# Reciprocal roots by GpSimd's power and one Newton step, squares summed into fewer tiles, last sample columns added on VectorE

## The chip, the cores and the metric

The kernel runs on one core of a Trainium2 chip. The metric is the device time of one execution in microseconds (us), lower being better. The engines in what follows are TensorE (PE; its weight loads are listed apart as PEld), VectorE (DVE), ScalarE (ACT), GpSimd (POOL) and SyncE (SP), which issues most DMAs.

## The reference

One step of a decoder with two layers of width 1024, over 512 prompt columns and 32 sample columns (8 sequences of 4 tokens). Layer 0 mixes with a gated linear attention (GLA), layer 1 with a forgetting attention (FoX) over keys and values that are projected once, between the layers.

```python
def rmsnorm(x, g):
    y = x * lax.rsqrt(jnp.mean(x * x, axis=-1, keepdims=True) + NORM_EPS)
    return y * g
def modulate(x, g, shift, scale):
    return rmsnorm(x, g) * (1 + scale[:, None, :]) + shift[:, None, :]
...
for layer in range(2):
    u = modulate(h, g_norm[layer, 0], ...); h = h + 0.5 * gate0 * swiglu(u, w_up0, w_down0)
    u = modulate(h, g_norm[layer, 1], ...); h = h + gate1 * mixer(u)
    u = modulate(h, g_norm[layer, 2], ...); h = h + 0.5 * gate2 * swiglu(u, w_up1, w_down1)
    if layer == 0:
        kvf = modulate(h, g_kv, ...) @ w_kvf      # then k = rmsnorm(k per head), v, logf
```

Reciprocal roots are needed for the adaptive norms (one set from the inputs and five from `h` after each block that follows; the norm of the shared keys and values and the one that opens layer 1 read the same `h` and share a set), and per head for the GLA output, the keys and the queries.

## The kernel before

The residual stream `h` lies in SBUF as 128 partitions x 8 blocks x 544 columns: the features are on partitions, the 512 prompt and 32 sample tokens are columns. The columns are worked in two halves of 272; the second ends with the 32 sample columns. Weights come from HBM in fp32 and are split into a high part (a cast on ScalarE) and a low part (a subtraction on VectorE, L158); every product is three matmuls (L176, L177, L178).

A feed-forward part ends with its last down projection, whose blocks run over `m` = 0 to 7 for the first half and then for the second. `residual` adds each block to `h` (VectorE, L393); in the second half the sample columns have gates of their own: `gs` on VectorE (L396), then the sum on GpSimd (L398). After the last contribution to a block, `square` squares its half on ScalarE (L346). The squares of blocks 1 to 5 are added on GpSimd (L350) to the tile of block 0; those of blocks 6 and 7 stay as tiles of their own. An output projection (`gwo` after GLA, `fwo` after FoX) ends in the same way.

When the eighth block of a half is there, `after` calls `stats`: matmuls with the tiles of squares as weights and a column of ones (L359) give the sums over the features, one token per partition, in three pieces (128, 128, 16 columns that count). `mean_eps` scales (L328, the tile `nx`), `rsqrt` takes the reciprocal root on VectorE (`nry`, `nrw`): an integer guess from the bits and three Newton steps, twelve instructions. `spread` puts each root on a diagonal (L336, `diag`, VectorE), and matmuls with ones (L337, `rb`) spread it over the partitions. From `rb` (copied to SBUF on ScalarE), `make_u` makes the next operand in two parts, `uh` (ScalarE) and `ul` (VectorE), block by block.

`norm_heads` normalises keys and queries per head: squares on ScalarE, a reduction and scaling on VectorE (`hss`, L1022 to L1024), `rsqrt` for 8 heads of a token block (`h8y`, `h8w`) or 2 of the samples (`h2y`), a product on VectorE (L1026) and one with the gain on GpSimd (L1027, `hxk`). It is called ten times for the keys and ten for the queries. The projection of keys and values (`kv`, L566 to L568) has the sample columns apart: `kv_s` (L554) with `us`, which GpSimd makes (L378).

Each engine runs its own queue in order; the order is fixed when the program is built, by a scheduler that places instructions by its own estimates of durations. SyncE's queue issues the loads of the weights, many blocks ahead.

Of the kernel before, what the change touches and what calls it, by code (L numbers as in the profile page):

```python
# [9 lines left out]
F32 = mybir.dt.float32  # L10
F32R = mybir.dt.float32r
BF16 = mybir.dt.bfloat16
I32 = mybir.dt.int32
U8 = mybir.dt.uint8
AF = mybir.ActivationFunctionType
ALU = mybir.AluOpType
AX = mybir.AxisListType

P = 128
D = 1024  # L20
NB = 8
TP = 512
NS = 32
T = TP + NS
# [5 lines left out]
MAGIC = 1597463007.0  # L30
# [69 lines left out]
def trunk_kernel(ctx: ExitStack, tc: tile.TileContext, a, out, dbg=None, stop=None):  # L100
    nc = tc.nc
    V, S, G, PE, SP = nc.vector, nc.scalar, nc.gpsimd, nc.tensor, nc.sync
    dbg = dbg or {}

    keep = ctx.enter_context(tc.tile_pool(name="keep", bufs=1))
# [4 lines left out]
    def mm_bank(name):  # L110
        return pp.tile([P, 512], F32, tag="mm", name=name, bufs=5)

    def aux_bank(name):
        return pp.tile([P, 512], F32, tag="aux", name=name, bufs=2)
# [14 lines left out]
    h = keep.tile([P, NB, T], F32, name="h")  # L129
# [10 lines left out]
    ones = cst[:, C_ONES:C_ONES + 128]  # L140


    def rsqrt(x, n, tag, rows=P):
        y = tmp.tile([P, n], F32, tag=tag + "y", name=tag + "y")
        w = tmp.tile([P, n], F32, tag=tag + "w", name=tag + "w")
        v, w = y[:rows], w[:rows]
        V.tensor_scalar(out=v.bitcast(I32), in0=x.bitcast(I32), scalar1=1, scalar2=None, op0=ALU.logical_shift_right)
        V.tensor_scalar(out=v.bitcast(I32), in0=v.bitcast(I32), scalar1=-1.0, scalar2=MAGIC, op0=ALU.mult, op1=ALU.add)
        V.tensor_scalar(out=x, in0=x, scalar1=-0.5, scalar2=None, op0=ALU.mult)
        for _ in range(3):  # L150
            V.tensor_tensor(out=w, in0=v, in1=v, op=ALU.mult)
            V.tensor_tensor(out=w, in0=w, in1=x, op=ALU.mult)
            V.scalar_tensor_tensor(out=v, in0=w, scalar=1.5, in1=v, op0=ALU.add, op1=ALU.mult)
        return y

    def halves(hi, lo, src):
# [130 lines left out]
    start = ExitStack()  # L287
# [22 lines left out]
    for t in range(5):  # L310
        n = P if t < 4 else NS
        V.tensor_tensor_reduce(out=junk[:n], in0=xt[t][:n], in1=xt[t][:n], scale=1.0, scalar=0.0, op0=ALU.mult, op1=ALU.add, accum_out=ss0[:n, t:t + 1])
    for k in range(NB):
        ps = mm_bank(f"xT{k}")
# [6 lines left out]
    ps = mm_bank("xTs")  # L321
# [4 lines left out]
    def mean_eps(name, src, n):  # L326
        x = tmp.tile([P, n], F32, tag="nx", name=name)
        V.tensor_scalar(out=x[:], in0=src, scalar1=1.0 / D, scalar2=EPS, op0=ALU.mult, op1=ALU.add)  # L328
        return x

    def spread(name, y, pieces):
        diag = tmp.tile([P, 3, P], F32, tag="diag", name=f"diag{name}", bufs=1)
        ps = aux_bank(f"rb{name}")
        b0 = pieces[0][3]
        for i, (col, k, r0, t0, n) in enumerate(pieces):
            V.tensor_scalar(out=diag[:k, i, :n], in0=cst[:k, C_ID + r0:C_ID + r0 + n], scalar1=y[:k, col:col + 1], scalar2=None, op0=ALU.mult)  # L336
            PE.matmul(ps[:, t0 - b0:t0 - b0 + n], lhsT=ones[:k, :], rhs=diag[:k, i, :n], start=True, stop=True)  # L337
        e = pieces[-1][3] + pieces[-1][4]
        S.copy(rb[:, b0:e], ps[:, 0:e - b0])

    accs = {}

    def square(m, half):
        t0, t1 = HALF[half]
        sq = tmp.tile([P, HA], F32, tag="acc" if m == 0 else "sq", name=f"sq{half}_{m}", bufs=2 if m == 0 else 3)
        S.activation(sq[:], h[:, m, t0:t1], AF.Square)  # L346
        if m == 0:
            accs[half] = [sq]
        elif m < NB - 2:
            G.tensor_tensor(out=accs[half][0][:], in0=accs[half][0][:], in1=sq[:], op=ALU.add)  # L350
        else:
            accs[half].append(sq)

    def stats(name, half):
        t0, t1 = HALF[half]
        ps = aux_bank(f"st{name}")
        for i, o in enumerate((0, 128, 144)):
            for j in range(3):
                PE.matmul(ps[:, i:i + 1], lhsT=accs[half][j][:, o:o + 128], rhs=ones[:, 0:1], start=j == 0, stop=j == 2)  # L359
        x = mean_eps(f"nx{name}", ps[:, 0:3], 3)  # L360
        y = rsqrt(x[:], 3, "nr")
        spread(name, y, [(0, P, 0, t0, 128), (1, P, 0, t0 + 128, 128), (2, P, 112, t0 + 256, 16)])

    def scaled(v, half, scale, k):
# [24 lines left out]
    def residual(name, ps, m, half, gate, last):  # L389
        t0, t1 = HALF[half]  # L390
        p1 = min(t1, TP)
        n = p1 - t0
        V.scalar_tensor_tensor(out=h[:, m, t0:p1], in0=ps[:, 0:n], scalar=mods[:, gate + m, 0:1], in1=h[:, m, t0:p1], op0=ALU.mult, op1=ALU.add)  # L393
        if half:
            st = tmp.tile([P, NS], F32, tag="gs", name=f"gs{name}_{m}", bufs=3)
            V.tensor_tensor(out=st[:].rearrange("p (s t) -> p s t", s=8), in0=ps[:, n:n + NS].rearrange("p (s t) -> p s t", s=8),  # L396
                            in1=mods[:, gate + m, 1:9].unsqueeze(2).to_broadcast([P, 8, 4]), op=ALU.mult)
            G.tensor_tensor(out=h[:, m, TP:T], in0=h[:, m, TP:T], in1=st[:], op=ALU.add)  # L398
        if last:
            square(m, half)  # L400

    def after(name, shift, scale):
        def f(half):
            stats(f"{name}{half}", half)
            if half:
                make_u(name, half, shift, scale)
                return []
            return [lambda k=k: make_u(name, half, shift, scale, k, k + 1) for k in range(NB)]
        return f
# [211 lines left out]

    x0 = mean_eps("nx0", ss0[:], 5)
    y0 = rsqrt(x0[:], 5, "n0")
    spread("0a", y0, [(0, P, 0, 0, 128), (1, P, 0, 128, 128)])
    spread("0b", y0, [(2, P, 0, 256, 128), (3, P, 0, 384, 128), (4, 32, 0, 512, 32)])
# [30 lines left out]
    def gla(after_half):  # L656
        W = a["gla_w_in"][0]
        with tc.tile_pool(name="gla", bufs=1) as gp:
# [199 lines left out]
            def normalise(name, po, n):  # L858
                ss = gp.tile([P, 4], F32, tag="oss", name=f"oss{name}", bufs=2)
                for i in range(n):  # L860
                    S.activation(jk, po(i), AF.Square, accum_out=ss[:, i:i + 1])
                V.tensor_scalar(out=ss[:, 0:n], in0=ss[:, 0:n], scalar1=1.0 / 256, scalar2=EPS, op0=ALU.mult, op1=ALU.add)
                y = rsqrt(ss[:, 0:n], n, f"o{n}")
                if len(ons) == 0:
                    on = onb
                else:
                    on = ada_tile(f"on{name}")[:].rearrange("p (h e) -> p h e", h=4)
                ons.append(on)
                for i in range(n):
                    if i % 2:  # L870
                        S.mul(on[:, i], po(i), y[:, i:i + 1])
                    else:
                        V.tensor_scalar(out=on[:, i], in0=po(i), scalar1=y[:, i:i + 1], scalar2=None, op0=ALU.mult)
# [591 lines left out]
```

## Time and profile before

| | us |
|---|---|
| median of three executions | 2459.07 (2456.82 to 2463.04) |
| profiled execution | 2463.23 |
| its span, first to last instruction | 2461.4 |
| TensorE busy / VectorE / ScalarE / GpSimd | 2391.6 / 1235.5 / 783.5 / 289.5 |
| mean granted clock of TensorE | 0.989 of full speed |

The busy times are shares of the span in which an engine executes; instructions of TensorE overlap, so a busy TensorE is not one at its peak. A row of the timeline has start, duration, engine, line, operation, output from inputs, shapes, and in brackets the idle time ahead of it with what ended that. A row of one source line has minimum, median and maximum duration in ns, and the starts of its first and last instruction.

### The profile page before, as it was taken

The numbers are of one execution on the slowest core, as the hardware profiler recorded it, in microseconds if no ns is written. First come the engines' busy times: TensorE is split into PE (matmuls) and PEld (weight loads), VectorE is DVE, ScalarE is ACT, GpSimd is POOL, SyncE is SP. The second block draws the span as 40 slices with busy tenths as digits, with TensorE's granted clock in tenths as the row PEclk, the third lists the DMA queues.
The fourth block names the chain that finished last, engine by engine and source line by source line (L and its number), as shares of the span: only waits on it lengthen the run. The fifth ranks groups of instructions, "written<-read, shape, count | busy, mean of one in ns | idle before, by whom it ended". The sixth has DMA issues, their size and how long they took to land. (4 is left out here: it accounts for less than half of the span.)

```text
span 2461.4 us, 48211 instructions
## 1 busy us (share of the span) xinstructions
PE 2391.6 (97%) x20204; PEld 2244.4 (91%) x20204; DVE 1235.5 (50%) x2823; ACT 783.5 (32%) x1431; POOL 289.5 (12%) x448
## 2 busy tenths in 40 slices
PE   7999999999899999999999999999999799999999
PEld 6999999988879999999979999999896579999999
DVE  6343334557656344344585344434847656444433
ACT  4212222344534213222334322222337444222221
POOL 0000000104302010000220000000325220000000
PEclk9999999999999999999999999999999899999999
DMA  9636454213172646554247323322157742222221
GB/s 308 232 126 231 156 178 133 65 48 96 36 215 60 224 145 230 179 176 154 97 125 233 99 66 109 97 92 69 44 109 196 177 129 74 91 88 93 70 85 54
DMA packets 325519, 319.38 MB, mean 130 GB/s; under 512 B 24607, under 2 KB 276349, under 8 KB 325254
## 3 DMA queue, kind: packets, MB, share of 16 engines
q1 hardware_dynamic: 297958, 293.81, 37.4%
q0 software_dynamic: 13776, 11.87, 2.3%
q10 hardware_dynamic: 13568, 10.62, 1.4%
q8 instruction: 159, 2.61, 0.4%
q14 instruction: 58, 0.48, 0.1%
HBM read 298.17 MB, written 18.38 MB: 129 GB/s over the span
## 5 line engine op out<-in xcount | busy, mean ns | idle before, releaser
L176 PE MATMUL pa<-uh,hua 128*128 128x272 f32 x1408 | 409.5, 291 | 2.0 <-ACT uh L386 2.0
L177 PE MATMUL pa<-ul,hua 128*128 128x272 f32 x1408 | 407.7, 290 | 0.4 <-DVE ul L387 0.2
L178 PE MATMUL pb<-uh,lub 128*128 128x272 f32 x1408 | 407.5, 289 | 0.0
L176 PE MATMUL pd<-gh,hwd 128*128 128x272 f32 x1408 | 407.4, 289 | 0.0
L178 PE MATMUL pa<-uh,lua 128*128 128x272 f32 x1408 | 406.6, 289 | 0.0
L176 PE MATMUL pb<-uh,hub 128*128 128x272 f32 x1408 | 405.5, 288 | 0.0
L177 PE MATMUL pb<-ul,hub 128*128 128x272 f32 x1408 | 405.5, 288 | 0.0
L177 PE MATMUL pd<-gl,hwd 128*128 128x272 f32 x1408 | 405.5, 288 | 0.0
L178 PE MATMUL pd<-gh,lwd 128*128 128x272 f32 x1408 | 405.2, 288 | 0.0
L393 DVE SCALAR_TENSOR_TENSOR h<-pd,mods,h 128x272 f32<-128x272 f32 (+1 forms) x384 | 185.2, 483 | 255.6 <-PE pd L178 254.4
L176 PEld LDWEIGHTS pa<-uh,hua 128*128 128x128 f32 x1408 | 265.3, 188 | 15.1 <-issue 6.0
L176 PEld LDWEIGHTS pd<-gh,hwd 128*128 128x128 f32 x1408 | 265.1, 188 | 2.9 <-issue 2.9
L177 PEld LDWEIGHTS pa<-ul,hua 128*128 128x128 f32 x1408 | 265.7, 189 | 1.4 <-DVE ul L387 1.2
L177 PEld LDWEIGHTS pb<-ul,hub 128*128 128x128 f32 x1408 | 266.1, 189 | 0.0
L178 PEld LDWEIGHTS pb<-uh,lub 128*128 128x128 f32 x1408 | 265.8, 189 | 0.0
L176 PEld LDWEIGHTS pb<-uh,hub 128*128 128x128 f32 x1408 | 265.7, 189 | 0.0
L177 PEld LDWEIGHTS pd<-gl,hwd 128*128 128x128 f32 x1408 | 265.5, 189 | 0.0
L178 PEld LDWEIGHTS pd<-gh,lwd 128*128 128x128 f32 x1408 | 265.4, 188 | 0.0
L178 PEld LDWEIGHTS pa<-uh,lua 128*128 128x128 f32 x1408 | 265.4, 188 | 0.0
L446 DVE TENSOR_TENSOR g<-g,pb 128x272 f32<-128x272 f32 x176 | 77.1, 438 | 346.5 <-PE pb L178 346.3
L157 ACT CAST hua<-rua 128x1024 fp32r<-128x1024 f32 x88 | 92.2, 1048 | 462.9 <-PE pd L177 352.0
L398 POOL TENSOR_TENSOR h<-h,gs 128x32 f32<-128x32 f32 x192 | 69.5, 362 | 1230.7 <-DVE gs L396 1214.6
(497 smaller groups left out, 4173.1 us busy)
## 6 DMA issues: line engine op xcount, KB each, us to landing
adaw<-in_w_ada_dram SPq DMA_DIRECT2D x128, 512.0 KB, 6.2
rua<-in_w_ffn_up_dram SPq DMA_DIRECT2D x88, 512.0 KB, 3.8
rub<-in_w_ffn_up_dram SPq DMA_DIRECT2D x88, 512.0 KB, 3.8
rwd<-in_w_ffn_down_dram SPq DMA_DIRECT2D x88, 512.0 KB, 5.3
adah<-in_w_ada_dram SPq DMA_DIRECT2D x16, 512.0 KB, 7.9
adaw<-in_w_ada_kv_dram SPq DMA_DIRECT2D x16, 512.0 KB, 7.3
s<-in_state_gla_dram SPq DMA_DIRECT2D x16, 512.0 KB, 6.2
kp<-in_cache_k_dram SPq DMA_DIRECT2D x16, 512.0 KB, 5.7
```

The costliest lines, as they stand in the source:

```text
L157: S.copy(hi, src)
L176: PE.matmul(ps, lhsT=wh, rhs=xh, start=first and i == 0, stop=False)
L177: PE.matmul(ps, lhsT=wh, rhs=xl, start=False, stop=False)
L178: PE.matmul(ps, lhsT=wl, rhs=xh, start=False, stop=last and i == n - 1)
L393: V.scalar_tensor_tensor(out=h[:, m, t0:p1], in0=ps[:, 0:n], scalar=mods[:, gate + m, 0:1], in1=h[:, m, t0:p1], op0=ALU.mult, op1=ALU.add)
L398: G.tensor_tensor(out=h[:, m, TP:T], in0=h[:, m, TP:T], in1=st[:], op=ALU.add)
L446: V.tensor_tensor(out=g[:], in0=g[:], in1=pb[:, 0:HA], op=ALU.mult)
```

## The change

The reciprocal root becomes a power of -1/2 on GpSimd, followed by one Newton step of four operations. In the norms (`stats`) that step runs on GpSimd too; elsewhere (start, GLA, keys, queries) on VectorE. In the first half all eight squares end in one tile, in the second seven in one and the eighth apart, and the statistics matmuls are three or six in place of nine. The last sum of the sample columns of a block goes to VectorE.

```diff
+    mhalf = keep.tile([P, 8], F32, name="mhalf")
+    V.memset(mhalf[:], -0.5)
+
-    def rsqrt(x, n, tag, rows=P):
+    def rsqrt(x, n, tag, rows=P, E=None):
+        E = E or V
         y = tmp.tile([P, n], F32, tag=tag + "y", name=tag + "y")
         w = tmp.tile([P, n], F32, tag=tag + "w", name=tag + "w")
         v, w = y[:rows], w[:rows]
-        V.tensor_scalar(out=v.bitcast(I32), in0=x.bitcast(I32), scalar1=1, scalar2=None, op0=ALU.logical_shift_right)
-        V.tensor_scalar(out=v.bitcast(I32), in0=v.bitcast(I32), scalar1=-1.0, scalar2=MAGIC, op0=ALU.mult, op1=ALU.add)
-        V.tensor_scalar(out=x, in0=x, scalar1=-0.5, scalar2=None, op0=ALU.mult)
-        for _ in range(3):
-            V.tensor_tensor(out=w, in0=v, in1=v, op=ALU.mult)
-            V.tensor_tensor(out=w, in0=w, in1=x, op=ALU.mult)
-            V.scalar_tensor_tensor(out=v, in0=w, scalar=1.5, in1=v, op0=ALU.add, op1=ALU.mult)
+        G.tensor_tensor(out=v, in0=x, in1=mhalf[:rows, 0:n], op=ALU.pow)
+        E.tensor_tensor(out=w, in0=v, in1=v, op=ALU.mult)
+        E.tensor_tensor(out=w, in0=w, in1=x, op=ALU.mult)
+        E.tensor_scalar(out=w, in0=w, scalar1=-0.5, scalar2=1.5, op0=ALU.mult, op1=ALU.add)
+        E.tensor_tensor(out=v, in0=w, in1=v, op=ALU.mult)
         return y
...
-        elif m < NB - 2:
+        elif m < NB - half:
             G.tensor_tensor(out=accs[half][0][:], in0=accs[half][0][:], in1=sq[:], op=ALU.add)
...
+        n = len(accs[half])
         for i, o in enumerate((0, 128, 144)):
-            for j in range(3):
-                PE.matmul(ps[:, i:i + 1], lhsT=accs[half][j][:, o:o + 128], rhs=ones[:, 0:1], start=j == 0, stop=j == 2)
+            for j in range(n):
+                PE.matmul(ps[:, i:i + 1], lhsT=accs[half][j][:, o:o + 128], rhs=ones[:, 0:1], start=j == 0, stop=j == n - 1)
         x = mean_eps(f"nx{name}", ps[:, 0:3], 3)
-        y = rsqrt(x[:], 3, "nr")
+        y = rsqrt(x[:], 3, "nr", E=G)
...
-            G.tensor_tensor(out=h[:, m, TP:T], in0=h[:, m, TP:T], in1=st[:], op=ALU.add)
+            (V if last else G).tensor_tensor(out=h[:, m, TP:T], in0=h[:, m, TP:T], in1=st[:], op=ALU.add)
```

The added lines shift what follows by two or three. The scheduler also orders the queues anew. Three places follow; a row gives the line, the operation, output from inputs (with the number of each tile's instance) and shape.

On VectorE after the first feed-forward part, first half (the norm's tiles are `nx`, `nry`, `nrw`, `diag`; `pd` are blocks of the down projection), before:

```order
L328 TENSOR_SCALAR nx_5138<-st_5128 128x3
L147 TENSOR_SCALAR nry<-nx_5138 128x3
L393 SCALAR_TENSOR_TENSOR h<-pd_18_0_1_5163,mods,h 128x240
L148 TENSOR_SCALAR nry<-nry 128x3
L149 TENSOR_SCALAR nx_5138<-nx_5138 128x3
L396 TENSOR_TENSOR gs_18_0_5177<-pd_18_0_1_5163,mods 128x32
L151 TENSOR_TENSOR nrw<-nry 128x3
L152 TENSOR_TENSOR nrw<-nrw,nx_5138 128x3
L153 SCALAR_TENSOR_TENSOR nry<-nrw,nry 128x3
```

and with the change:

```order
L396 SCALAR_TENSOR_TENSOR h<-pd_18_0_1_5147,mods,h 128x240
L330 TENSOR_SCALAR nx_5129<-st_5125 128x3
L399 TENSOR_TENSOR gs_18_0_5161<-pd_18_0_1_5147,mods 128x32
L401 TENSOR_TENSOR h<-h,gs_18_0_5161 128x32
L338 TENSOR_SCALAR diag_5138<-cst,nry 128x128 x2
L338 TENSOR_SCALAR diag_5138<-cst,nry 128x16
```

Before, the last three rows come twice more, among them further blocks of the second half, ahead of the diagonal; now the diagonal follows `nx` after the first block's sample columns, and the root is GpSimd's, whose queue at this place now reads:

```order
L352 TENSOR_TENSOR sq_0_5004<-sq_0_5004,sq_6_5105 128x272
L352 TENSOR_TENSOR sq_0_5004<-sq_0_5004,sq_7_5122 128x272
L151 TENSOR_TENSOR nry<-nx_5129,mhalf 128x3
L152 TENSOR_TENSOR nrw<-nry 128x3
L153 TENSOR_TENSOR nrw<-nrw,nx_5129 128x3
L154 TENSOR_SCALAR nrw<-nrw 128x3
L155 TENSOR_TENSOR nry<-nrw,nry 128x3
L352 TENSOR_TENSOR sq_0_5164<-sq_0_5164,sq_1_5183 128x272
```

The squares of blocks 6 and 7 are added, then come the power and its Newton step, and the sums of the second half's squares behind them. On TensorE at the same place, before:

```order
L359 MATMUL st_5128<-cst,sq_0_5009 128x1
L359 MATMUL st_5128<-cst,sq_6_5110 128x1
L176 MATMUL pd_18_0_1_5163<-gh_18_4162,hwd_18_4973 128x272
L177 MATMUL pd_18_0_1_5163<-gl_18_4163,hwd_18_4973 128x272
L178 MATMUL pd_18_0_1_5163<-gh_18_4162,lwd_18_4974 128x272
```

and with the change:

```order
L178 MATMUL pd_18_0_1_5147<-gh_21_4851,hwd_21_4986 128x272
L179 MATMUL pd_18_0_1_5147<-gl_21_4852,hwd_21_4986 128x272
L180 MATMUL pd_18_0_1_5147<-gh_21_4851,lwd_21_4987 128x272
L362 MATMUL st_5125<-cst,sq_0_5004 128x1 x3
L178 MATMUL pd_18_1_1_5166<-gh_18_4157,hwd_18_4968 128x272
```

Two statistics matmuls stood ahead of the second half's first block and seven after its ninth matmul, and 28 matmuls led from there to `rb`; now all three stand behind that block's twelve matmuls, and 13 lead to `rb`. On TensorE at the norm ahead of keys and values, second half, before:

```order
L337 MATMUL rbkv_13742<-diagkv_13741,cst 128x128 x2
L337 MATMUL rbkv_13742<-diagkv_13741,cst 128x16
L566 MATMUL kv_1_14044<-hkv_3_13993,uh 128x512
L567 MATMUL kv_1_14044<-lkv_3_13994,uh 128x512
L568 MATMUL kv_1_14044<-hkv_3_13993,ul 128x512
L554 MATMUL kv_s<-rkv_0_13973,us 32x128 x8
```

and with the change:

```order
L570 MATMUL kv_0_13897<-lkv_3_13894,uh 128x512
L339 MATMUL rbkv_13642<-diagkv_13641,cst 128x128 x2
L339 MATMUL rbkv_13642<-diagkv_13641,cst 128x16
L571 MATMUL kv_0_13897<-hkv_3_13893,ul 128x512
L569 MATMUL kv_0_13897<-hkv_3_13893,uh 128x512
```

`rb` stood behind nearly all of the projection's block `kv_1`, three matmuls ahead of `kv_s`; now it stands in the block `kv_0`, and 25 matmuls lead from it to `kv_s`.

## The prediction

> **What bounds the kernel.** I read first the page's busy times and its row of the granted clock.
>
> ```profile
> PE 2391.6 (97%) x20204; PEld 2244.4 (91%) x20204; DVE 1235.5 (50%) x2823; ACT 783.5 (32%) x1431; POOL 289.5 (12%) x448
> PEclk9999999999999999999999999999999899999999
> ```
>
> TensorE is busy for 97% of the span. So the change can gain only by giving TensorE fewer instructions, shorter waits, or a clock that falls less often. Second came the list of what TensorE waits for (us in total, times, longest), of which these rows belong to the norms, the K stage and the projections that follow a norm:
>
> ```profile
> PE st L359 <- POOL sq L350: 2.6, 2, 1.3
> PE st L359 <- ACT sq L346: 2.0, 4, 0.7
> PE kv L566 <- ACT hkv L157: 2.0, 2, 1.5
> PE pa L176 <- ACT uh L386: 2.0, 3, 1.4
> PE kv_s L554 <- POOL us L378: 1.9, 1, 1.9
> PE stkv L359 <- POOL sq L350: 1.3, 1, 1.3
> PE gq L176 <- ACT uh L386: 0.4, 1, 0.4
> ```
>
> Nothing in it names a tile of the start's norm, of the GLA norms or of the Q stage. Third, short windows behind five of these waits; the columns are us, busy PE, PEld, DVE, ACT and POOL with counts, then the granted clock, DMA share and GB/s.
>
> ```profile
> 480.50:483.90 3.40, 3.40 (x18) 3.40 (x17) 1.99 (x4) 2.88 (x5) 0.00 (x0) 0.51 0.07 9
> 777.40:781.00 3.60, 3.60 (x19) 3.60 (x18) 2.66 (x12) 2.52 (x7) 0.00 (x0) 0.53 0.82 236
> 1227.00:1231.00 4.00, 4.00 (x26) 3.56 (x25) 2.99 (x6) 1.18 (x3) 0.00 (x0) 1.00 0.00 0
> 1241.50:1245.00 3.50, 3.50 (x65) 3.12 (x66) 3.50 (x11) 2.39 (x6) 0.00 (x0) 0.54 0.42 103
> 1288.00:1292.00 4.00, 2.85 (x11) 2.40 (x12) 3.96 (x6) 0.61 (x2) 1.81 (x1) 0.69 0.22 66
> ```
>
> After some waits the clock is halved for about 3.4 us: a dip. The lost time is the window times one minus the clock: 3.40 x 0.49 = 1.7 us, 3.60 x 0.47 = 1.7, 3.50 x 0.46 = 1.6, and 4.00 x 0.31 = 1.2. The third window, after a wait of 1.3 us (stkv on POOL), kept the full clock. So a wait of this size brings a dip at some places and not at others.
>
> **Term A, fewer statistics matmuls.** There are 144 + 36 = 180 instructions, 18 for each of ten calls:
>
> ```profile
> L359 PE MATMUL st<-cst,sq x144: 164/250/352, 461.9 to 2054.6; 128*128 128x1 f32 x144
> L359 PE MATMUL stkv<-cst,sq x36: 164/250/272, 1208.0 to 1229.7; 128*128 128x1 f32 x36
> ```
>
> A call issues three columns times three tiles, nine matmuls of two instructions. Now the first half has three matmuls and the second six, so 6 and 12 instructions and 90 over five norms. The other 90 go. Their price follows from the timeline of the norm after the first feed-forward part, first half:
>
> ```profile
> 460.29 0.77 POOL L350 TENSOR_TENSOR sq<-sq,sq 128x272 f32<-128x272 f32 x1 [0.74 <-ACT sq L346]
> 462.72 0.43 ACT L346 ACTIVATE sq<-h 128x272 f32<-128x272 f32 x1 [1.08 <-DVE h L393]
> 463.50 1.62 PE L359 MATMUL st<-cst,sq 128*128 128x1 f32 x14
> 464.98 0.37 PE L176 MATMUL pd<-gh,hwd 128*128 128x272 f32 x1
> 465.15 0.17 DVE L328 TENSOR_SCALAR nx<-st 128x3 f32<-128x3 f32 x1 [2.53 <-PE st L359]
> 468.41 1.13 DVE L336 TENSOR_SCALAR diag<-cst,nry 128x128 f32<-128x128 f32 x3
> 468.75 1.24 PE L337 MATMUL rb<-diag,cst 128*128 128x128 f32 x6
> 469.84 0.38 PE L177 MATMUL pd<-gl,hwd 128*128 128x272 f32 x1
> ```
>
> Fourteen take 464.98 - 463.50 = 1.48 us, 0.106 each; 90 x 0.106 = **-9.5 us**, all on TensorE's path.
>
> **The price of pow (x).** No row shows GpSimd's power. The bounds come from GpSimd's own rows:
>
> ```profile
> L398 POOL TENSOR_TENSOR h<-h,gs x192: 243/254/1277, 122.1 to 2454.5; 128x32 f32<-128x32 f32 x192
> L350 POOL TENSOR_TENSOR sq<-sq,sq x50: 757/774/1417, 454.1 to 2046.3; 128x272 f32<-128x272 f32 x50
> L967 POOL TENSOR_TENSOR km<-kstk,cst x4: 1888/1897/1897, 795.8 to 1094.2; 96x1024 fp32r<-96x1024 f32 x4
> ```
>
> The line through 254 ns at 32 columns and 774 at 272 meets zero columns near 0.19 us: the low end, a pow as cheap as a product. The high end is GpSimd's longest arithmetic row, 1.9 us. I take x = 0.4, nearest to the rows of few columns, doubled for a costlier function. For the four Newton operations that stay on GpSimd in the norms I take 0.25 each.
>
> **Term B, first halves.** Now all eight tiles of squares must be in one before the first statistics matmul. The last square ends on ScalarE at 462.72 + 0.43 = 463.15; GpSimd starts 0.15 later (ScalarE to GpSimd, as at 460.29) and ends at 464.07. TensorE now has twelve matmuls of the next block before it (at 0.125, the step of neighbouring rows) and is there at 463.4: a wait of 0.7 us where there was none. Six instructions (0.64) and a drain of 0.14 later, nx, pow, Newton and the three diag rows follow: nx begins at 464.93 and pow at 465.18; the diag rows begin at 466.25 + x, and 1.43 us later (468.41 to 469.84 before) rb is done, at 467.68 + x. TensorE without a wait would be there after 464.76 + 13 x 0.125 + 0.64 = 467.02: a wait of 0.66 + x = 1.06. Before, 28 matmuls and 0.64 led from 464.98 to 469.12, rb's end was 469.84: 0.72. So +0.7 + 1.06 - 0.72 = 1.0, three times. After an output projection ten matmuls instead of 13 cover it, and before there was next to no wait:
>
> ```profile
> 762.33 0.28 PE L177 MATMUL gwo<-ul,hgwo 128*128 128x272 f32 x1
> 762.63 0.84 PE L337 MATMUL rb<-diag,cst 128*128 128x128 f32 x6
> 763.33 0.37 PE L178 MATMUL gwo<-uh,lgwo 128*128 128x272 f32 x1
> ```
>
> (763.33 - 762.33 - 0.125 - 0.64 = 0.2.) That gives 0.7 + 1.43 - 0.2 = 1.9, twice. **Together +6.8 us.** Ends: x at 0.19 and at 1.9 makes it 5 x 0.2 = 1.0 less and 5 x 1.5 = 7.5 more. Behind the waiting matmuls stand the next blocks of the down projection, whose results VectorE takes only after the diag rows; behind pow stand GpSimd's sums of the second half, which start later than these blocks end, so nobody else waits. The move of the last sample columns to VectorE adds to it a 128x32 row between nx and diag, beside GpSimd's chain: nothing while that chain is longer.
>
> **Term C, second halves.** Before, the statistics waited 2.6 + 2.0 + 1.3 = 5.9 us, uh behind it 2.0 + 0.4, and two dips cost 3.4: 11.7. Now:
>
> ```profile
> 478.76 0.38 PE L359 MATMUL st<-cst,sq 128*128 128x1 f32 x2 [1.26 <-POOL sq L350]
> 481.28 1.21 DVE L158 TENSOR_TENSOR lgq<-rgq,hgq 128x1024 fp32r<-128x1024 f32 x1
> ```
>
> VectorE's own add spares the sample columns a change of engine, so I halve the 1.26 to 0.6 for three norms, and take 0.4 after the output projections. Then the chain to rb: drain 0.14, nx 0.17, change 0.08, pow 0.4, Newton 1.0, and, since the diag rows stand behind a 1024-column subtraction on VectorE, up to its 1.21, then 1.43: 4.4 us. Against it stand 17 matmuls and rb's own 0.64, 2.8 us (20 after an output projection, 3.1): waits of 1.7 and 1.3. So 3 x 2.3 + 2 x 1.7 = 10.3, and **-1.4 us**. Ends: -7.4 if the subtraction runs beside GpSimd at all five places, +1.9 if the statistics wait as before (5.9 instead of 2.6).
>
> **Term D, kv_s.** Here 3 matmuls stood between rb and kv_s, now 25 do:
>
> ```profile
> 1241.45 3.41 PE L554 MATMUL kv_s<-rkv,us 128*32 128x128 f32 x64 [1.86 <-POOL us L378]
> ```
>
> 22 more matmuls of 512 columns, at over the 0.125 of 272 columns, cover the 1.86 (2.8 us and more), and with it goes the dip of 1.6: **-3.5 us** (ends -3.5 and 0).
>
> **Term E, K stage.** VectorE fills it, and TensorE waits behind casts:
>
> ```profile
> 1285.35 0.17 DVE L151 TENSOR_TENSOR h8w<-h8y 128x8 f32<-128x8 f32 x1
> 1285.55 0.17 DVE L152 TENSOR_TENSOR h8w<-h8w,hssk 128x8 f32<-128x8 f32 x1
> 1287.02 0.43 PE L566 MATMUL kv<-hkv,uh 128*128 128x352 f32 x1 [1.50 <-ACT hkv L157]
> 1288.75 0.43 PE L567 MATMUL kv<-lkv,uh 128*128 128x352 f32 x1 [1.30 <-DVE lkv L158]
> 1290.64 0.66 PE L567 MATMUL kv<-lkv,uh 128*128 128x352 f32 x1 [0.40 <-DVE lkv L158]
> ```
>
> Ten head norms lose 12 - 4 operations of 0.20 us each, 16 us of VectorE's work. Waits of 1.50 + 1.30 + 0.40 and a dip of 1.2 make 4.4; I leave 0.4 of it: **-4.0 us** (ends -4.4, and 0 where pow queues behind GpSimd's products in the stage and VectorE waits for it as long as it saves; one or two VectorE rows stand between and cover it). In the Q stage as much work goes, but there TensorE does not wait though VectorE is full:
>
> ```profile
> 1760.00:1780.00 20.00, 20.00 (x147) 16.19 (x146) 20.00 (x80) 9.39 (x17) 5.20 (x3) 1.00 0.31 107
> ```
>
> So nothing there, and nothing for start and GLA (no wait of theirs above). No DMA is added; on SP's queue only two loads change places, which costs nothing while the loads run blocks ahead.
>
> **Term F, dips again.** Two of five second halves had one. With waits still as long, I keep that rate: **+3.4 us**. First halves get none: their two waits are each shorter than 1.26, the shortest before a dip above, and the 0.72 at 468.75 left the clock whole:
>
> ```profile
> 460.00:480.00 20.00, 18.45 (x144) 17.61 (x143) 14.63 (x46) 7.94 (x19) 8.14 (x19) 1.00 0.01 2
> ```
>
>
> Sum: -9.5 + 6.8 - 1.4 - 3.5 - 4.0 + 3.4 = -8.2 us, from the profiled 2463.2 (span 2461.4 and 1.8 around it) to 2455.0. That execution stands 4.2 above the median of the runs, 2459.07; on the median's basis **2451 us**, -0.33%. About 0.3% (7.4 us) is what a measurement can tell from no change.
>
> Two pages weigh otherwise. By the Trainium skill, "GPSIMD Engine Reference", section "Engine selection", elementwise work belongs on VectorE, with GpSimd some two times slower for two inputs; here the 128x32 row above (0.254 against 0.17 for VectorE's nx) shows 1.5 times. By the page the sum would be rival (1)'s second, -4.6 instead of -8.2. By "TensorE: Matmul & The Clock Gate" of the Trainium skill (section HAM oscillation — how this bites in real kernels), "The abstract rule is "no PE-idle gaps >~3.4µs.""; this trace differs, a 1.26-us wait stands ahead of a window at 0.51. By the rule term F would be nothing, and the sum -11.6.
>
> **The rivals.** (1) No change: dips fall behind half of the ten chains of norms (five, 8.5 us instead of 3.4), -8.2 + 5.1 = -3.1, 2456; or GpSimd takes 0.34, twice VectorE's 0.17, for each of the 40 Newton rows: 3.6 us more, 2454.5. For the first: first halves get new waits; against: a wait of 0.72 brought no dip. For the second: GpSimd's rows reach 1277 ns; against: their median of 254. (2) Slower, by a slow pow: ten rb chains and ten head norms of the K stage all wait for it, 20 us per us of x. The gain is eaten at x = 0.4 + 8.2 / 20 = 0.8; from 1.2 it is slower by over 0.3%; at 1.9 it is 2451 + 30 = 2481. For it: no row shows the function; against: few columns are cheap in every row. (3) More gain: the subtraction is hidden at all second halves and no dip is left: -8.2 - 6.0 - 3.4 = -17.6, 2441.
>
> **Chances.** Forecast 0.43, (1) 0.33, (2) 0.18, (3) 0.06. Half of a slow pow's cases end above 2474. The range is 2441 to 2474. Faster 0.48, same 0.34, slower 0.18.
>
> **What would show it.** 90 statistics instructions; GpSimd rows of pow near 0.4; rb waits of about a microsecond in all ten calls; kv_s and the K stage without waits; two dips. It is wrong if pow takes over 0.8 us, if the statistics wait more than 0.7 in first halves, or if every rb wait is followed by a dip.

## The result and the profile after

The changed kernel is slower: 2479.28 us in the median of six executions (2470.07 to 2482.51) against 2460.92 for the kernel before (2456.82 to 2465.85); the ratio is 1.0067, 95% interval 1.0052 to 1.0082. The forecast of 2451 was wrong in sign, and the time lies outside the range. The profiled execution took 2477.44 us, its span 2475.3.

The page of the changed kernel, its busy times and its row of the granted clock:

```profile
PE 2385.8 (96%) x20114; PEld 2237.4 (90%) x20114; DVE 1200.6 (49%) x2536; ACT 784.6 (32%) x1431; POOL 346.2 (14%) x499
PEclk9999999989999999999999999999999899999999
```

TensorE has exactly 90 instructions fewer and VectorE 35 us less work, as the change promises; GpSimd has 57 us more. The rows of GpSimd's power (minimum, median and maximum duration in ns):

```profile
L151 POOL TENSOR_TENSOR nry<-nx,mhalf x8: 863/1334/1796, 467.9 to 2069.5; 128x3 f32<-128x3 f32 x8
L151 POOL TENSOR_TENSOR h8y<-hssk,mhalf x8: 1629/1636/1863, 1249.1 to 1300.9; 128x8 f32<-128x8 f32 x8
L151 POOL TENSOR_TENSOR o4y<-ossc,mhalf x4: 1006/1010/1024, 665.4 to 693.4; 128x4 f32<-128x4 f32 x4
L151 POOL TENSOR_TENSOR h2y<-hssks,mhalf x2: 696/698/701, 1254.2 to 1288.3; 128x2 f32<-128x2 f32 x2
L151 POOL TENSOR_TENSOR o1y<-osss,mhalf x1: 570/570/570, 711.5 to 711.5; 128x1 f32<-128x1 f32 x1
```

From one column to eight the time rises from 0.57 to 1.64 us, so by 0.15 us a column on a base of 0.42. The forecast had taken 0.4 for all of them. What TensorE waits for now, the rows that belong to the change:

```profile
PE rb L339 <- DVE diag L338: 9.2, 8, 1.6
PE st L362 <- POOL sq L352: 7.2, 8, 1.8
PE kv L570 <- DVE lkv L160: 5.2, 3, 3.0
PE stkv L362 <- POOL sq L352: 2.7, 2, 2.2
PE rbkv L339 <- DVE diagkv L338: 2.3, 2, 1.3
PE fq L570 <- DVE lfq L160: 2.1, 2, 1.6
PE kv L569 <- ACT hkv L159: 1.8, 1, 1.8
```

For the casts and low parts of `kv` that is 7.0 us. Before it was 3.7: 2.0 for the casts (in the list ahead of the forecast) and

```profile
PE kv L567 <- DVE lkv L158: 1.7, 2, 1.3
```

What VectorE waits for now:

```profile
DVE h8w L152 <- POOL h8y L151: 25.5, 16, 1.9
DVE diag L338 <- POOL nry L155: 15.4, 8, 2.1
```

All sixteen roots of eight columns have VectorE standing still, 1.6 us each. How that reaches TensorE is seen best at its longest wait in the K stage:

```profile
1262.41 1.63 POOL L151 TENSOR_TENSOR h8y<-hssk,mhalf 128x8 f32<-128x8 f32 x1
1264.07 0.17 DVE L152 TENSOR_TENSOR h8w<-h8y 128x8 f32<-128x8 f32 x1 [1.95 <-POOL h8y L151]
1264.64 1.22 DVE L160 TENSOR_TENSOR lkv<-rkv,hkv 128x1024 fp32r<-128x1024 f32 x1
1265.92 0.79 PE L570 MATMUL kv<-lkv,uh 128*128 128x512 f32 x1 [2.98 <-DVE lkv L160]
```

VectorE stands still for 1.95 us until the power ends at 1264.04, the low part `lkv` stands behind it in VectorE's queue, and TensorE waits 2.98 us for `lkv`. The kernel before has no wait of TensorE here. Another norm of the stage can be compared step by step:

```profile
1293.46 0.16 DVE L1027 TENSOR_SCALAR hssk<-hssk 128x8 f32<-128x8 f32 x1
1293.70 1.64 POOL L151 TENSOR_TENSOR h8y<-hssk,mhalf 128x8 f32<-128x8 f32 x1 [2.49 <-DVE hssk L1027]
1295.37 0.17 DVE L152 TENSOR_TENSOR h8w<-h8y 128x8 f32<-128x8 f32 x1 [1.75 <-POOL h8y L151]
1295.98 0.17 DVE L155 TENSOR_TENSOR h8y<-h8w,h8y 128x8 f32<-128x8 f32 x1
1297.72 0.43 PE L570 MATMUL kv<-lkv,uh 128*128 128x352 f32 x1 [1.57 <-DVE lkv L160]
```

From the end of scaling at 1293.62 to the root at 1296.15 it takes 2.5 us. The first and the last of the twelve operations at the same norm of the kernel before:

```profile
1284.94 0.17 DVE L147 TENSOR_SCALAR h8y<-hssk 128x8 int32<-128x8 int32 x1
1286.95 0.17 DVE L153 SCALAR_TENSOR_TENSOR h8y<-h8w,h8y 128x8 f32<-128x8 f32 x1
```

They took 2.2 us. So the chain did not get shorter; VectorE only waits through its first two thirds instead of computing. Behind it stand the low parts of the weights (`lkv`), and TensorE waits 1.57 us for them, where it had waited 1.30. (The wait for a cast just ahead, 1.76 us after 1.50, is not this power's: the cast starts at 1294.90, before the power ends.)

What a stage lasts can be read from the first and last start of the keys' and the queries' matmuls. Before, and with the change:

```profile
L566 PE MATMUL kv<-hkv,uh x160: 311/325/662, 1225.1 to 1341.4; 128*128 128x512 f32 x64, 128*128 128x352 f32 x64, 128*128 128x336 f32 x32
L566 PE MATMUL fq<-hfq,uh x64: 388/393/496, 1746.4 to 1799.1; 128*128 128x512 f32 x64
```

```profile
L569 PE MATMUL kv<-hkv,uh x160: 312/326/642, 1227.4 to 1351.1; 128*128 128x512 f32 x64, 128*128 128x352 f32 x64, 128*128 128x336 f32 x32
L569 PE MATMUL fq<-hfq,uh x64: 387/395/501, 1754.2 to 1812.6; 128*128 128x512 f32 x64
```

The K stage went from 116.3 to 123.7 us (+7.4), the Q stage from 52.7 to 58.4 (+5.7). Not all of that is the power per head. In the Q stage TensorE's waits are 1.81 us for squares (until 1757.31) and 1.61 for rb (until 1764.45), which belong to the norm ahead of it, and 1.58 and 0.56 for low parts behind the power (until 1789.64 and 1791.86). The K stage holds such a norm too, and dips of the clock:

```profile
1230.00:1234.00 4.00, 3.12 (x8) 2.58 (x9) 2.84 (x5) 1.51 (x3) 0.83 (x1) 0.59 0.01 3
1264.00:1271.00 7.00, 5.08 (x13) 3.91 (x14) 5.81 (x13) 1.07 (x2) 2.73 (x3) 0.56 0.24 74
1298.00:1305.00 7.00, 6.33 (x25) 5.97 (x25) 4.80 (x10) 0.94 (x2) 3.14 (x3) 0.57 0.53 147
```

The first holds one dip, the windows of 7 us at 0.56 and 0.57 two each. The first stands at a wait of 2.18 us for squares (until 1230.88), the second at the 2.98 us above, the third behind the 1.57. Over the whole run the mean granted clock is 0.981 to 0.986 in the six executions, 0.983 in the mean; in 86 executions of the kernel before that ran beside the experiments it is 0.9868. A difference of 0.0035 over 2460 us is 8.6 us. By this estimate 8.6 of the 18 us are lost in dips. The waits cost more than the rest, since the smaller number of statistics matmuls gives part of it back: in the profiled executions TensorE's idle time (span less busy time) is 89.5 us, against 69.8 before.

### The profile page after: what moved, and what is told of

Its sections match the earlier page's. It is cut to its first block, busy times and chain, and to the rows that moved or that the text cites. A ratio compares the mean times of both kernels' runs of the same rounds, so it can differ in the third digit from the quotient of the medians.

```text
span 2475.3 us, 47832 instructions
## 1 busy us (share of the span) xinstructions
PE 2385.8 (96%) x20114; PEld 2237.4 (90%) x20114; DVE 1200.6 (49%) x2536; ACT 784.6 (32%) x1431; POOL 346.2 (14%) x499
## 4 chain that ended last, share of the span: by engine, by line
PE 83%; DVE 6%; DMA 4%; POOL 3%; ACT 2%; issue 1%; SPq 0%; ACTq 0%; POOLq 0%; DVEq 0%
PE pa L178 7%; PE pa L179 7%; PE pa L180 7%; PE pb L178 7%; PE pb L180 7%; PE pb L179 7%; PE pd L178 7%; PE pd L180 7%; PE pd L179 7%; PE ada L233 3%; DMA kd<-khscr 2%; PE kv L570 1%; PE kv L571 1%; PE kv L569 1%; DVE nv L370 1%
## 5 line engine op out<-in xcount | busy, mean ns | idle before, releaser
L401 POOL TENSOR_TENSOR h<-h,gs 128x32 f32<-128x32 f32 x168 | 60.8, 362 | 1205.3 <-DVE gs L399 1205.3
```

The costliest lines, as they stand in the source:

```text
L401: (V if last else G).tensor_tensor(out=h[:, m, TP:T], in0=h[:, m, TP:T], in1=st[:], op=ALU.add)
```

## The experiments

All ratios are against executions of the kernel before on the same chip, with 95% intervals. Experiment 4 is a probe that is read by its rows alone.

| kernel | median, us | ratio | mean clock |
|---|---|---|---|
| the change | 2479.3 | 1.0067 (1.0052 to 1.0082) | 0.983 |
| 1 old root, other parts kept | 2460.0 | 0.9987 (0.9972 to 1.0003) | 0.986 |
| 2 power in the norms only | 2466.9 | 1.0017 (1.0004 to 1.0030) | 0.986 |
| 3 power per head and at the start only | 2470.2 | 1.0035 (1.0021 to 1.0049) | 0.986 |
| 5 a product in the power's place | 2456.8 | 0.9979 (0.9966 to 0.9993) | 0.985 |
| 6 a second power per head | 2502.2 | 1.0160 (1.0142 to 1.0177) | 0.982 |
| 7 the power alone | 2471.9 | 1.0041 (1.0025 to 1.0058) | 0.985 |
| 8 old root, two tiles of squares in both halves | 2466.2 | 1.0018 (1.0001 to 1.0034) | 0.985 |
| 9 shorter root on VectorE, other parts kept | 2455.3 | 0.9971 (0.9958 to 0.9984) | 0.987 |
| 10 shorter root alone | 2455.6 | 0.9978 (0.9964 to 0.9992) | 0.987 |
| 11 sums on VectorE alone | 2459.0 | 0.9994 (0.9979 to 1.0009) | 0.988 |
| 12 merged squares alone | 2469.7 | 1.0031 (1.0018 to 1.0044) | 0.983 |

**Theory and rival.** Theory 1: the power's length is what costs, since VectorE (per head) and TensorE (at rb) stand behind it. Theory 2: merging the squares, and the order of the queues that comes with it, is what costs.

**1. The old root, the other parts kept.** `rsqrt_bits` is the root of the kernel before.

```diff
-        y = rsqrt(x[:], 3, "nr", E=G)
+        y = rsqrt_bits(x[:], 3, "nr")
...
-        y = rsqrt(ss, nh, f"h{nh}")
+        y = rsqrt_bits(ss, nh, f"h{nh}")
```

(and so at the start and in GLA.)

> The reciprocal root is VectorE's twelve operations again at all places; the merged squares and the sums of the last sample columns on VectorE stay as in the change. Theory 1 (GpSimd's power is what costs, 0.57 us at one column to 1.64 at eight, because VectorE stands still behind it in the K, Q and GLA stages): without it the other two parts keep their gain, 90 statistics instructions fewer, so 2448 to 2456 us, 0.2 to 0.5% below the kernel before. Theory 2 (merging the squares is what costs, since the first statistics matmul waits for a longer chain of sums, 9.9 us of waits against 5.9): 2465 to 2475, slower than before though no power is left.

2459.95 us, 0.13% below the kernel before, which is not told from no change: the loss went with the power, but the gain that theory 1 added for the other parts is not there in full (2448 to 2456 was expected). The K stage lasts 116.8 us again. The waits for squares stayed:

```profile
PE st L375 <- POOL sq L365: 6.7, 8, 1.3
PE stkv L375 <- POOL sq L365: 1.7, 2, 1.2
PE rb L352 <- DVE diag L351: 1.1, 3, 0.5
```

Those for rb fell from 11.5 to 1.1. With the old root the scheduler also leaves 31 matmuls between the statistics and rb in the first half after the feed-forward part, where the change has 13.

**2. The power in the norms only.** The heads are shown; start and GLA are edited alike.

```diff
-        y = rsqrt(ss, nh, f"h{nh}")
+        y = rsqrt_bits(ss, nh, f"h{nh}")
```

> The power and its Newton step on GpSimd only in the ten statistics calls of the norms; start, GLA, keys and queries have VectorE's twelve operations. Theory 1: the ten calls wait for rb, 11.5 us in the changed kernel, against 9.5 us of statistics matmuls saved; 2455 to 2463, no change that can be told. Theory 2 (merged squares and the norms' chains cost): about 2475, as slow as the changed kernel.

2466.86 us, +0.17%: above the range of theory 1, below that of theory 2. Against experiment 1 the power in the ten statistics calls costs 0.30%, 7.4 us. The waits for rb are back (7.6 + 2.3 us).

**3. The power per head and at the start only.** 

```diff
-        y = rsqrt(x[:], 3, "nr", E=G)
+        y = rsqrt_bits(x[:], 3, "nr")
```

> The power only at the start and per head (GLA, keys, queries); the norms have VectorE's twelve operations. Theory 1: VectorE still waits 1.6 us for each of sixteen powers of eight columns and TensorE behind it in the K and Q stages, so 2466 to 2474, most of the loss. Theory 2: 2450 to 2456, since the norms' chains are as before.

2470.18 us, +0.35%, where theory 1 put it. Against experiment 1 that is 0.48%, 11.8 us. The two costs, 0.30 and 0.48%, add up to nearly the 0.80% between experiment 1 and the change. The K stage lasts 122.3 us, the Q stage 57.4. The length of the Q stage does not tell the two apart, though: it is 59.0 us in experiment 2, which has no power per head, at a granted clock of 0.91 in the stage. GLA cannot be read in this way either: its `gv` matmuls span 61.0 us before, 65.1 with the change, 64.9 with the old root, and vary with its dips.

**4. Probes of the power.** Powers of known values, products, all ahead of the kernel before:

```diff
+        for value in (1.0, 0.001, 1000.0, 3.7):
+            V.memset(prbx[:], value)
+            for n in (1, 3, 8, 32):
+                G.tensor_tensor(out=prby[:, 0:n], in0=prbx[:, 0:n], in1=prbm[:, 0:n], op=ALU.pow)
+        for n in (3, 8, 32):
+            G.tensor_tensor(out=prby[:, 0:n], in0=prbx[:, 0:n], in1=prbm[:, 0:n], op=ALU.mult)
```

> The kernel before with a set of probes ahead of it: powers of 1, 3, 8 and 32 columns on GpSimd, each for the values 1, 0.001, 1000 and 3.7, products of 3, 8 and 32 columns on GpSimd and on VectorE, and three powers of 3 columns that start with no VectorE work, with a 512-column product of two SBUF operands, and with one of one operand, beside them. If the power costs by the column: 0.40 + 0.154 us per column (0.57 at one, 0.86 at 3, 1.64 at 8), so about 5.3 at 32, the same for all four values. If the 1.79 us of the second halves come from the values, the powers of 0.001 or 1000 take twice the time; if they come from VectorE's two-operand work beside them, the second of the last three powers is longer by most of that work's duration, the third is not.

The powers of values in the timeline:

```profile
2.65 9.63 POOL L153 TENSOR_TENSOR prby<-prbx,prbm 128x1 f32<-128x1 f32 x4 [2.20 <-DVE prbx L151]
12.52 9.74 POOL L153 TENSOR_TENSOR prby<-prbx,prbm 128x1 f32<-128x1 f32 x4 [0.24 <-DVE prbx L151]
22.50 9.72 POOL L153 TENSOR_TENSOR prby<-prbx,prbm 128x1 f32<-128x1 f32 x4 [0.24 <-DVE prbx L151]
32.45 9.72 POOL L153 TENSOR_TENSOR prby<-prbx,prbm 128x1 f32<-128x1 f32 x4 [0.24 <-DVE prbx L151]
```

The rows by line of the products and of the last three powers:

```profile
L155 POOL TENSOR_TENSOR prby<-prbx,prbm x3: 196/205/252, 42.2 to 42.8; 128x3 f32<-128x3 f32 x1, 128x8 f32<-128x8 f32 x1, 128x32 f32<-128x32 f32 x1
L164 POOL TENSOR_TENSOR prby<-prbx,prbm x3: 850/851/855, 45.9 to 48.2; 128x3 f32<-128x3 f32 x3
```

Each of the four rows of the timeline groups the four sizes for one value: 9.6 to 9.7 us whatever the value, so the values do not set the time. Taken apart, a power takes 0.86 us at three columns, 1.64 at eight and 5.43 at 32 (5.70 for the first value), as the slope would have it. The first of each group, of one column, takes 1.56 us (1.20 for the first value), against 0.57 in the changed kernel; why was not settled. A product takes 0.20 us at 3 columns and 0.25 at 32; a power of 3 takes 0.85. (VectorE's products that were to run beside the last three powers were scheduled far ahead of them, so these rows say nothing on the 1.79 us.)

**5. A product in the power's place.**

```diff
-        G.tensor_tensor(out=v, in0=x, in1=mhalf[:rows, 0:n], op=ALU.pow)
+        G.tensor_tensor(out=v, in0=x, in1=mhalf[:rows, 0:n], op=ALU.mult)
...
-        E.tensor_scalar(out=w, in0=w, scalar1=-0.5, scalar2=1.5, op0=ALU.mult, op1=ALU.add)
-        E.tensor_tensor(out=v, in0=w, in1=v, op=ALU.mult)
+        E.tensor_scalar(out=w, in0=w, scalar1=0.0, scalar2=0.6, op0=ALU.mult, op1=ALU.add)
+        E.tensor_tensor(out=v, in0=w, in1=w, op=ALU.mult)
```

> The changed kernel with every power replaced by a product on the same operands (0.20 us in the probe for 3 to 8 columns), the last Newton rows fed with a constant so that numbers stay finite; the order of all queues is that of the changed kernel. The roots are not computed. Theory 1 (the power's length alone is what costs): VectorE no longer stands still behind GpSimd in the K, Q and GLA stages and the rb waits shrink by 0.7 us each: 2450 to 2458, near what was forecast. Theory 2 (the new order of the queues, the handing to and fro between VectorE and GpSimd, or the merged squares cost): 2468 or more.

2456.78 us, 0.21% below the kernel before and 0.9% below the change, with the same order of the instructions on every engine. VectorE's wait for GpSimd and TensorE's for rb shrank as the operation did:

```profile
L151 POOL TENSOR_TENSOR h8y<-hssk,mhalf x8: 196/206/408, 1244.7 to 1286.2; 128x8 f32<-128x8 f32 x8
L151 POOL TENSOR_TENSOR nry<-nx,mhalf x8: 192/656/1120, 468.7 to 2044.3; 128x3 f32<-128x3 f32 x8
DVE h8w L152: 3.7, 11
```

(the last row is from the list of who waited for these operations: 3.7 us in eleven cases, against 25.5 in sixteen), and of TensorE's waits:

```profile
PE rb L339 <- DVE diag L338: 3.8, 8, 1.0
PE st L362 <- POOL sq L352: 7.2, 8, 1.8
```

TensorE's idle time is 69.5 us, as before the change (69.8), against 89.5 with the power. The K stage lasts 111.9 us, 4.4 less than before; its waits for casts and low parts of `kv` (3.7 us before) and the one for kv_s (1.9) are gone, and a wait of 2.17 us for squares lies in it. The waits for squares did not move at all, so they are not the power's. Nor are most of the dips: the mean clock is 0.9848, against 0.9833 with the power and 0.9868 before. Theory 2 as the chief cause falls: with all else in place, the power's length alone is worth 0.9%.

**6. A second power per head.** In `norm_heads` ahead of the root:

```diff
+        yy = tmp.tile([P, nh], F32, tag=f"hh{nh}", name=f"hh{nh}")
+        G.tensor_tensor(out=yy[:], in0=ss, in1=mhalf[:, 0:nh], op=ALU.pow)
         y = rsqrt(ss, nh, f"h{nh}")
```

> The changed kernel with a second power of the same columns ahead of the one that is used, in the twenty head norms of keys and queries only (16 of 8 columns, 4 of 2: 16 x 1.64 + 4 x 0.70 = 29 us of GpSimd work). Theory 1: the first powers cost some 10 of their 29 us in these two stages; the second ones find no cover left and cost more, 15 to 29 us: 2494 to 2508. Theory 2: GpSimd is idle for over 80% of the span and takes them beside other work: 2479 to 2484.

2502.22 us, 22.9 above the change for 29 us of added GpSimd work, in the middle of theory 1's range.

```profile
DVE h8w L152 <- POOL h8y L151: 51.8, 16, 3.5
PE kv L570 <- DVE lkv L160: 9.3, 6, 4.3
PE fq L570 <- DVE lfq L160: 6.2, 2, 5.2
```

VectorE's standstill doubled from 25.5 us to 51.8, and the K and Q stages went to 134.7 and 68.4 us. An engine that is idle for some 85% of the span has little slack here, because another engine's queue stands behind it.

**7. The power alone.** Squares and sums as before:

```diff
-        elif m < NB - half:
+        elif m < NB - 2:
...
-            (V if last else G).tensor_tensor(out=h[:, m, TP:T], in0=h[:, m, TP:T], in1=st[:], op=ALU.add)
+            G.tensor_tensor(out=h[:, m, TP:T], in0=h[:, m, TP:T], in1=st[:], op=ALU.add)
```

> Only the reciprocal root is changed (power and Newton step, on GpSimd in the norms); the squares stay in three tiles and the last sums of the sample columns on GpSimd, as before. Theory 1: the root costs 15 to 20 us in itself and the other two parts gain 3 to 8: 2475 to 2485. Theory 2 (the merged squares are what costs): 2460 to 2466.

2471.91 us, +0.41%, a little below the range: the power costs some 10 us alone, and not 15 to 20. The other two parts do not gain on top of it, the change with all three is slower still: beside them the power costs twice as much (0.80% against experiment 1). Why the two add up to more was not settled.

**8. Two tiles in both halves.** On experiment 1:

```diff
-        elif m < NB - half:
+        elif m < NB - 1:
```

> VectorE's old root at all places, sums of the last sample columns on VectorE, and squares in two tiles in both halves (the eighth block's apart), so that the first halves' statistics need not wait for GpSimd's last sum. If that wait (0.5 to 0.9 us at five places) costs more than three more matmuls (0.64 us), 2453 to 2458, faster than the kernel before; if the two weigh the same, 2458 to 2462, as with one tile.

2466.21 us, +0.18%, outside both ranges. The waits for squares are no smaller (7.5 + 2.2 us): those on `st` are six in place of eight, but the longest is 2.8 us in place of 1.3.

**9. A shorter root on VectorE.** On experiment 1, other constants for the guess, two Newton steps:

```diff
-        V.tensor_scalar(out=v.bitcast(I32), in0=v.bitcast(I32), scalar1=-1.0, scalar2=MAGIC, op0=ALU.mult, op1=ALU.add)
-        V.tensor_scalar(out=x, in0=x, scalar1=-0.5, scalar2=None, op0=ALU.mult)
-        for _ in range(3):
-            V.tensor_tensor(out=w, in0=v, in1=v, op=ALU.mult)
-            V.tensor_tensor(out=w, in0=w, in1=x, op=ALU.mult)
-            V.scalar_tensor_tensor(out=v, in0=w, scalar=1.5, in1=v, op0=ALU.add, op1=ALU.mult)
+        V.tensor_scalar(out=v.bitcast(I32), in0=v.bitcast(I32), scalar1=-1.0, scalar2=1595932665.0, op0=ALU.mult, op1=ALU.add)
+        V.tensor_scalar(out=x, in0=x, scalar1=-0.703952253, scalar2=None, op0=ALU.mult)
+        V.tensor_tensor(out=w, in0=v, in1=v, op=ALU.mult)
+        V.tensor_tensor(out=w, in0=w, in1=x, op=ALU.mult)
+        V.scalar_tensor_tensor(out=v, in0=w, scalar=1.6819141, in1=v, op0=ALU.add, op1=ALU.mult)
+        V.tensor_tensor(out=w, in0=v, in1=v, op=ALU.mult)
+        V.scalar_tensor_tensor(out=w, in0=w, scalar=0.71027544, in1=x, op0=ALU.mult, op1=ALU.mult)
+        V.scalar_tensor_tensor(out=v, in0=w, scalar=1.5, in1=v, op0=ALU.add, op1=ALU.mult)
```

> The bits' guess with other constants and two Newton steps on VectorE at all places, nine operations instead of twelve (largest relative error 7e-7 in a host estimate over random numbers); merged squares and the last sums on VectorE as in the change. Theory 1 (what counts is VectorE's time per root, 2.4 us for twelve operations, while the power adds 1.6 us of standstill to four): 26 roots lose 0.6 us each, of which the K, Q and GLA stages show a part: 2 to 6 us below the version with the old root, 2452 to 2458. Rival: VectorE is no longer waited for in those stages with the old root (its K stage takes 0.6 us more than before the change), so nothing is gained, 2458 to 2462.

2455.25 us, 0.29% below the kernel before: faster than both kernels and in theory 1's range. It is 4.7 us below experiment 1 in the medians, but the intervals of the two overlap, so a gain over the old root beside the merged squares is not shown.

**10. The shorter root alone.** The root of experiment 9 and, as in experiment 7, squares and sums as before:

```diff
-        elif m < NB - half:
+        elif m < NB - 2:
...
-            (V if last else G).tensor_tensor(out=h[:, m, TP:T], in0=h[:, m, TP:T], in1=st[:], op=ALU.add)
+            G.tensor_tensor(out=h[:, m, TP:T], in0=h[:, m, TP:T], in1=st[:], op=ALU.add)
```

> The nine-operation root alone; squares in three tiles and the last sums on GpSimd as before. Theory 1: 2455 to 2461, 0.1 to 0.3% below the kernel before. If the merged squares bring 3 us of their own, this is 3 us above the version that has both.

2455.55 us, 0.22% below the kernel before: here the shorter root is the only edit, and it gains. It gives most of what experiment 9 has; the intervals overlap, so the rest of the change is not shown to add anything to it.

**11. The sums on VectorE alone.** On experiment 1:

```diff
-        elif m < NB - half:
+        elif m < NB - 2:
```

> Only the sums of the last blocks' sample columns go to VectorE; root and squares as before. They take a change of engine out of the chain to the last squares (up to 0.3 us at each of five second halves): 2460 to 2463, no change that can be told.

2459.02 us, no change that can be told (0.9994, 0.9979 to 1.0009).

**12. The merged squares alone.** On experiment 1:

```diff
-            (V if last else G).tensor_tensor(out=h[:, m, TP:T], in0=h[:, m, TP:T], in1=st[:], op=ALU.add)
+            G.tensor_tensor(out=h[:, m, TP:T], in0=h[:, m, TP:T], in1=st[:], op=ALU.add)
```

> Only the squares are merged (90 statistics instructions fewer, 9.5 us by their step); root and sums as before. If TensorE's step is all, 2453 to 2456; if the later first statistics matmul gives most of it back (8.4 us of waits against 5.9 in the version with the old root, and clock dips behind them), 2457 to 2462.

2469.66 us, +0.31%: slower, which neither expectation had. The 90 instructions go, but the waits and the clock take back more:

```profile
PE st L375 <- POOL sq L365: 6.1, 8, 2.0
PE st L375 <- ACT sq L361: 2.9, 2, 1.5
PE stkv L375 <- POOL sq L365: 2.4, 2, 1.9
```

That is 11.4 us, with the sums still on GpSimd, against 8.4 with them on VectorE (experiment 1) and 5.9 before. The mean clock is 0.9833 against 0.9868, 8.6 us by the same estimate as above, more than the whole loss. So the merging loses with the sums on GpSimd, and together with the sums on VectorE (experiment 1) it gains nothing that can be told. Why the dips follow these waits and not others was not settled.

## Why the prediction was wrong

- **The step that failed: the price of pow.** It was taken as x = 0.4, "nearest to the rows of few columns, doubled for a costlier function". It is 0.57 at one column, 0.86 at three and 1.64 at eight. The bounds, 0.19 and 1.9, held it. The choice between them went by GpSimd's products, whose time hardly depends on the columns (0.20 us at 3, 0.25 at 32); the power's does, 0.15 us for each. One x for all sizes, taken near the low end, was the error, and rival (2), slower by a slow pow, is what happened. Its slope (20 us per us of x, break-even at 0.8, slower from 1.2) gave 2481 at x = 1.9; with the measured 1.64 and 0.70 for the heads (eight and two columns) and 0.86 for the norms it would have been 2451 + 8 x 1.24 + 2 x 0.30 + 10 x 0.46 = 2466. That has the right sign and is still 13 us short; the clock and the terms below hold the rest, which was not divided further.
- **The cover, term E.** One or two VectorE rows were to hide a power of 0.4 in the K stage. They cannot hide 1.64: VectorE stood still 1.6 us at each. The term was -4.0. TensorE's waits for casts and low parts of `kv` went from 3.7 us to 7.0 instead; at 0.2 us they are gone (experiment 5), so the term was sound for a fast power. The length of the stage is no measure of it, since it also holds kv_s, a norm and dips: in experiment 7, with the power at its full length, it is 116.8 us.
- **The Q stage, put at nothing.** TensorE did not wait there, though VectorE was full; that it would stay so was right for less work on VectorE and wrong for a standstill: 2.1 us of waits for `lfq`. The rest of the 5.7 us by which the stage is longer is the norm's (1.81 and 1.61).
- **Term A** was right as a count, 90 instructions. That it is a gain of 9.5 us was not: alone the merged squares lose 0.31%.
- **Terms B and C.** The waits for rb were forecast at 3 x 1.06 + 2 x 1.43 + 3 x 1.7 + 2 x 1.3 = 13.7 us and are 11.5. That they lie so near is luck. The forecast had x = 0.4; with the measured 0.86 in the first and 1.79 in the second halves its sum would have been some 23, and at 0.2 us it would have been 11.7, where experiment 5 has 4.1. The chain around the power was priced too high, and the power too low. The waits for squares were forecast at 5 x 0.7 + 3 x 0.6 + 2 x 0.4 = 6.1 and are 9.9: the sum over seven squares in the second half ends later than assumed, 2.18 us after TensorE is there at worst (keys and values).
- **Term D** was right, kv_s is waited for no more.
- **Term F** had too few dips. Terms C to F together took 2.8 us of dips out of the sum (3.4 + 1.6 + 1.2 less 3.4). A profile of the kernel before has 25 us of them, one of the change 36, and by the mean clock over all executions the change has 8.6 us more. Which of the new waits bring them was not settled.
- In the second halves the power takes 1.79 us instead of 0.86. It starts beside VectorE's subtraction:

```profile
487.72 0.16 DVE L330 TENSOR_SCALAR nx<-st 128x3 f32<-128x3 f32 x1 [2.52 <-PE st L362]
487.80 1.23 DVE L160 TENSOR_TENSOR lgq<-rgq,hgq 128x1024 fp32r<-128x1024 f32 x1
487.96 1.79 POOL L151 TENSOR_TENSOR nry<-nx,mhalf 128x3 f32<-128x3 f32 x1 [4.90 <-DVE nx L330]
490.88 0.63 DVE L338 TENSOR_SCALAR diag<-cst,nry 128x128 f32<-128x128 f32 x3 [1.86 <-POOL nry L155]
491.22 0.84 PE L339 MATMUL rb<-diag,cst 128*128 128x128 f32 x6 [1.30 <-DVE diag L338]
```

The excess, 0.93 us, is the same for the product of experiment 5 (0.19 to 1.12), so it is not the power's; 487.80 + 1.23 - 487.96 = 1.07 us of the subtraction lay ahead of it. The Trainium skill, "SBUF — State Buffer", section "SBUF: two separate sides", has a rule for this: a VectorE instruction with two SBUF inputs and a GpSimd instruction that reads SBUF share a pair of interfaces, and the one that starts later waits for all of the other. The trace agrees to 0.14 us. The forecast had put this subtraction in the chain at up to its full 1.21, as a row ahead of the diagonal: nearly right in size, by another path.
- The rule of "GPSIMD Engine Reference", section "Engine selection", in the Trainium skill (two times slower for elementwise work with two inputs) did not decide either: a Newton product of three columns took 0.19 us on GpSimd, where VectorE takes 0.16. The forecast's 1.5 times set a sum of 32 columns against a scaling of three; the same sum of 32 columns takes 0.25 us on GpSimd and 0.18 on VectorE in the changed kernel. It is the power, which VectorE was not doing, that was slow.

## What to carry to other kernels

An operation that no row of the trace shows is to be priced at every size in which it will run, and the forecast is to be made at both ends; here the probe's few rows would have turned the sign of the forecast. Before an operation is moved to an idle engine, look at who stands behind its result: here VectorE's in-order queue stood still for 25.5 us behind 26 us of power per head, and idle time of the helper was little cover (22.9 us lost for 29 us added). And fewer instructions on the busiest engine gained nothing here, where the first of them had to wait longer.

## What had not been expected of the hardware

- GpSimd's power costs about 0.42 us and 0.15 more for each column, in the changed kernel's rows of one to eight columns and in the probe's of 3, 8 and 32 for each of the values tried, against 0.20 us for a product of up to eight. The probe's power of one column, at 1.56 us, does not fit.
- The scatter of one kernel's times goes with the granted clock: in the twelve executions of the version with the shorter root, 2447 us at 0.989 and 2461 at 0.983. Comparing mean clocks told a loss by dips (merged squares alone, 0.983) from a loss by waiting (power per head, 0.986).
